# The input product of a ConvFFN by a seven-factor 2x2 block product, its activations held in DRAM

## The chip, the cores and the metric

The kernel runs on one core of one Trainium2 chip. The metric is the device time of one execution in microseconds (us). A core has five engines that each work through a queue of their own in order: TensorE (PE; the loading of its weights is shown as PEld), VectorE (DVE), ScalarE (ACT), GpSimd (POOL) and SyncE (SP, which here issues DMA transfers). They wait for one another by semaphores. SBUF is the core's memory for operands, PSUM the memory that PE writes its products to.

## The reference

One step of a hybrid layer: modulation, stick-breaking attention, a short gated convolution, a merge with an output projection, and then a feed-forward part with a convolution in it. The change concerns the last part:

```
h2 = modulate(rms_norm(x, g_norm2), shift2, scale2)
up, gate = jnp.split(h2 @ w_up, 2, axis=-1)
up_c, new_ffn = causal_dwconv(up, ffn_prev, w_fconv, b_fconv)
x = x + gate2[:, None, :] * ((jax.nn.silu(up_c) * gate) @ w_down)
```

There are 512 prompt tokens and 32 sample tokens, 1024 features, and 2816 features in the feed-forward part. All is float32.

## The kernel before

Every activation is kept with features on the partitions (128) and the T = 544 tokens as columns, in two halves of HT = 272. 1024 features are KD = 8 tiles, the 2816 are KF = 22. A float32 product is made of three products of a faster format: weights and activations are each split into a high and a low part (`split`, L91 on ACT for the high part, L92 on DVE for the low one; for weights `load_w`, L96 the transfer by SP, L99 the cast on ACT, L100 the subtraction on DVE), and `mm3` runs high by high, high by low and low by high for each contraction tile k and each half: 8 x 3 x 2 = 48 matmuls of 272 columns for a product with one weight tile.

After the output projection, `h2` makes the second norm's output for one half of the columns at a time: a product on POOL (L679), scale and shift on DVE (L682), the split into `h2h` and `h2l`. PE fills the time with the last projection tiles (`out_half`) and the first three FFN products (`up_half`: the up tiles of f = 0 and 1, the gate tile of f = 0).

The loop over f in 0..21 then does, for each tile of 128 features, the up product (48 matmuls), copies it from PSUM to `up` on ACT (L732), pads it and saves its last rows on POOL (L441 to L446), runs three taps of the convolution on DVE (L451, L453), silu on ACT (L735), the gate product (48 matmuls), multiplies the two on DVE (L739, into `gf`) and splits the result into `fh` and `fl`, which stay in SBUF. The down product follows: eight output tiles of 22 x 6 = 132 matmuls, with weights by `load_w`; the last tile is done by halves, so that the final norm of one half runs beside the other's product.

A list scheduler puts the instructions of the program on the engines' queues, so the order in the queues is not always that of the code. Tile pools with a number of buffers (`bufs`) set how far ahead an engine may run.

Of the kernel before, what the change touches and what calls it, by code (L numbers as in the profile page):

```python
# [34 lines left out]
# Token columns of every [feature, token] tile, as two halves, the latest token first:  # L35
# prompt 511..256 | sample 31..16, prompt 255..0 | sample 15..0.
# [4 lines left out]
# Columns of the per-partition vectors that are packed into one array.  # L41
# [9 lines left out]
def build(tc, a):  # L51
    nc = tc.nc
    ctx = ExitStack()
    with ctx:
# [4 lines left out]
        # ---------------------------------------------------------------- constants  # L59
# [65 lines left out]
        def proj(w, x):  # L125
            """Product with a weight tile, in DRAM or loaded."""
# [6 lines left out]
        def steps(src, post, lo):  # L133
            """The product of x with a weight tile in steps, and what follows it."""
# [10 lines left out]
        def fill(n):  # L145
            """n steps of the products that wait in the queue."""
# [7 lines left out]
        def after(inst, earlier):  # L154
            """Order two instructions of one engine."""
# [3 lines left out]
        def log_tables(earlier):  # L159
            """Load the table set that has Ln and Exp, after an activation that needs another one."""  # L160
# [6 lines left out]
        def rstd_of(pool, ss_ps, y, tables):  # L167
            """y = (mean + eps) ** -0.5 of the column sums in psum, in every partition."""
# [5 lines left out]
            # one Newton step: y * (1.5 - 0.5 v y y)  # L174
# [9 lines left out]
        # ---------------------------------------------------------------- adaLN  # L184
# [9 lines left out]
        def dot(raw, sums):  # L194
            """Each row of raw times silu(c), summed."""
# [4 lines left out]
        def ada(s, t):  # L200
            """mods[:, s, t, :]: one feature tile of one of the last four modulations, both batches."""
# [9 lines left out]
        # ---------------------------------------------------------------- first norm, first projections  # L211
# [6 lines left out]
        def flat(ps, name):  # L218
            """psum to [p, T] with all prompt columns first."""
# [9 lines left out]
        def queries(j, ps):  # L229
            """A head's (hi, lo) over each other, hi on the head's own partitions."""  # L230
# [7 lines left out]
        def keys(j, ps):  # L238
            """A head's (hi, hi) and (lo, lo)."""
# [16 lines left out]
        def values_t(j):  # L256
            """[keys, quarters]: head 0 hi, lo; head 1 lo, hi."""
# [11 lines left out]
        # sample queries, keys and values of all heads, kept until all are there  # L269
# [32 lines left out]
        def mod(s, k, on_pe):  # L302
            """mods[:, s, k, :]: one feature tile of one of the first two modulations."""
# [41 lines left out]
        # ---------------------------------------------------------------- projections and prompt attention  # L345
# [18 lines left out]
        def causal(t, width, fill):  # L364
            """Fill where the key is not before the query: [queries, blocks of width keys], last key first."""
# [4 lines left out]
        def scores(j, e):  # L370
            """One head's weights for the prompt: queries on partitions, keys from the last one back."""
# [27 lines left out]
        def transposed(sg):  # L399
            """The weights with keys on partitions, split, by rows of key blocks."""  # L400
# [441 lines left out]
```

## Time and profile before

| | us |
|---|---|
| median of 3 runs | 1123.93 |
| lowest and highest run | 1121.76, 1124.09 |
| span of the profiled execution | 1122.7 |
| PE busy | 1053.6 (94%) |
| DVE busy | 666.1 (59%) |
| ACT busy | 428.6 (38%) |
| POOL busy | 262.4 (23%) |

The span is the time from the first to the last recorded instruction of the profiled execution; of that execution no other time is recorded, and the median of the runs is 1.2 us above its span. Busy shares are averages over stages that differ: the attention lies in the first half, the FFN in the last 400 us. PE's matmuls overlap one another, so the duration of one (0.29 us) is longer than the distance between two.

### The profile page before, as it was taken

The numbers are of one execution on the slowest core, as the hardware profiler recorded it, in microseconds if no ns is written. First come the engines' busy times: TensorE is split into PE (matmuls) and PEld (weight loads), VectorE is DVE, ScalarE is ACT, GpSimd is POOL, SyncE is SP. The second block draws the span as 40 slices with busy tenths as digits, with TensorE's granted clock in tenths as the row PEclk, the third lists the DMA queues.
The fourth block names the chain that finished last, engine by engine and source line by source line (L and its number), as shares of the span: only waits on it lengthen the run. The fifth ranks groups of instructions, "written<-read, shape, count | busy, mean of one in ns | idle before, by whom it ended". The sixth has DMA issues, their size and how long they took to land.

```text
span 1122.7 us, 19599 instructions
## 1 busy us (share of the span) xinstructions
PE 1053.6 (94%) x8042; PEld 1027.6 (92%) x8042; DVE 666.1 (59%) x1005; ACT 428.6 (38%) x749; POOL 262.4 (23%) x384
## 2 busy tenths in 40 slices
PE   3898888898999999999999999899999999999995
PEld 1688787887999999999999999899999999999995
DVE  6967787776775534666677756755455455422334
ACT  5466566565643322222222253333333333322230
POOL 3434455443321101211211215300010010001112
PEclk9899999999999999999999999899999999999998
DMA  9612121211122222455455463022222222222212
GB/s 372 217 40 95 58 78 50 73 61 67 68 88 73 79 73 94 152 187 175 165 182 178 167 228 115 1 74 78 95 91 79 95 93 77 87 90 85 85 53 80
DMA packets 38153, 120.60 MB, mean 107 GB/s; under 512 B 4272, under 2 KB 7472, under 8 KB 37936
## 3 DMA queue, kind: packets, MB, share of 16 engines
q1 hardware_dynamic: 37920, 119.22, 30.9%
q8 instruction: 63, 1.03, 0.4%
q10 hardware_dynamic: 144, 0.14, 0.1%
q14 instruction: 26, 0.21, 0.1%
HBM read 112.60 MB, written 6.75 MB: 106 GB/s over the span
## 4 chain that ended last, share of the span: by engine, by line
PE 79%; DVE 10%; ACT 4%; issue 3%; POOL 2%; DMA 1%; DVEq 0%; SPq 0%; ACTq 0%; POOLq 0%
PE ps L112 72%; DVE keep L392 3%; PE o L362 2%; PE at L408 1%; POOL keep L367 1%; DVE hf L682 1%; DVE sg L393 1%; ACT keep L388 1%; DVE adum L197 1%; PE slot L112 1%; DVE kt L246 1%; DMA cbc<-in_c_dram 1%; ACT wh L99 1%; PE so L362 1%; ACT sg L389 1%
## 5 line engine op out<-in xcount | busy, mean ns | idle before, releaser
L99 ACT CAST wh<-raw 128x1024 fp32r<-128x1024 f32 x153 | 159.7, 1045 | 349.0 <-PE ps L112 246.0
L100 DVE TENSOR_TENSOR wl<-raw,wh 128x1024 fp32r<-128x1024 f32 (+1 forms) x120 | 146.4, 1222 | 169.6 <-ACT wh L99 169.0
L112 PE MATMUL ps<-hh,wh 128*128 128x272 f32 x992 | 212.0, 295 | 8.1 <-ACT qs L235 8.1
L112 PE MATMUL ps<-hl,wh 128*128 128x272 f32 x992 | 206.8, 290 | 0.0
L112 PE MATMUL ps<-hh,wl 128*128 128x272 f32 x992 | 206.6, 290 | 0.0
L112 PEld LDWEIGHTS ps<-hh,wh 128*128 128x128 f32 x992 | 157.9, 191 | 11.0 <-ACT qs L235 9.6
L112 PEld LDWEIGHTS ps<-hl,wh 128*128 128x128 f32 x992 | 157.8, 191 | 0.0
L112 PEld LDWEIGHTS ps<-hh,wl 128*128 128x128 f32 x992 | 156.9, 191 | 0.0
L112 PE MATMUL ps<-h2l,wh 128*128 128x272 f32 x704 | 150.6, 290 | 0.9 <-DVE h2l L92 0.9
L112 PE MATMUL ps<-h2h,wh 128*128 128x272 f32 x704 | 150.9, 290 | 0.3 <-ACT h2h L91 0.3
L112 PE MATMUL ps<-h2h,wl 128*128 128x272 f32 x704 | 151.1, 291 | 0.0
L100 POOL TENSOR_TENSOR wl<-raw,wh 128x1024 fp32r<-128x1024 f32 x33 | 81.9, 2481 | 203.9 <-ACT wh L99 194.3
L112 PEld LDWEIGHTS ps<-h2l,wh 128*128 128x128 f32 x704 | 113.4, 190 | 1.7 <-DVE h2l L92 1.7
L112 PEld LDWEIGHTS ps<-h2h,wh 128*128 128x128 f32 x704 | 113.6, 190 | 0.9 <-ACT h2h L91 0.8
L112 PEld LDWEIGHTS ps<-h2h,wl 128*128 128x128 f32 x704 | 112.6, 190 | 0.0
L197 DVE SCALAR_TENSOR_TENSOR adum<-araw,cbc 128x1024 f32<-128x1024 f32 x64 | 82.7, 1293 | 41.8 <-DMA araw<-in_w_ada_dram 41.0
L392 DVE TENSOR_TENSOR_SCAN keep<-keep,zero 128x512 f32<-128x512 f32 (+1 forms) x64 | 65.9, 1041 | 8.1 <-POOL keep L367 6.3
L112 PE MATMUL ps<-fl,wh 128*128 128x272 f32 x308 | 63.9, 288 | 0.0
L367 POOL TENSOR_SCALAR_AFFINE_SELECT keep<-keep 128x128 f32<-128x128 f32 x64 | 44.3, 693 | 83.5 <-issue 43.7
L112 PE MATMUL ps<-fh,wh 128*128 128x272 f32 x308 | 63.6, 288 | 0.0
L112 PE MATMUL ps<-fh,wl 128*128 128x272 f32 x308 | 63.5, 288 | 0.0
L662 POOL TENSOR_TENSOR sacc<-sacc,sq 128x272 f32<-128x272 f32 x24 | 27.5, 1162 | 143.3 <-ACT sq L660 143.3
(200 smaller groups left out, 1745.6 us busy)
## 6 DMA issues: line engine op xcount, KB each, us to landing
raw<-in_w_in_dram SPq DMA_DIRECT2D x64, 512.0 KB, 3.3
raw<-in_w_up_dram SPq DMA_DIRECT2D x44, 512.0 KB, 3.3
araw<-in_w_ada_dram SPq DMA_DIRECT2D x32, 512.0 KB, 4.0
raw<-in_w_down_dram SPq DMA_DIRECT2D x16, 512.0 KB, 3.5
mraw<-in_w_ada_dram SPq DMA_DIRECT2D x10, 512.0 KB, 7.3
raw<-in_w_branch_b_dram SPq DMA_DIRECT2D x8, 512.0 KB, 3.2
raw<-in_w_branch_a_dram SPq DMA_DIRECT2D x8, 512.0 KB, 3.3
raw<-in_w_out_dram SPq DMA_DIRECT2D x8, 512.0 KB, 3.8
```

Of the source, the lines that this page charges most:

```text
L99: nc.scalar.copy(wh[:, :nk], raw[:, :nk])
L100: lo.tensor_tensor(wl[:, :nk], raw[:, :nk], wh[:, :nk].bitcast(F32), ALU.subtract)
L112: nc.tensor.matmul(ps[:, i, 0:c1 - c0], w[:, k], x[:, k0 + k, c0:c1], start=s, stop=e)
L197: nc.vector.scalar_tensor_tensor(adum, raw, 1.0, cbc[:, n], ALU.mult, ALU.mult, accum_out=sums[:, n:n + 1])
L246: nc.vector.tensor_tensor(kt[s, e, 1], kf[s], kt[s, e, 0].bitcast(F32), ALU.subtract)
L362: nc.tensor.matmul(out, l, r, start=s, stop=t, skip_group_check=True)
L367: nc.gpsimd.affine_select(out=t, in_=t, pattern=pat, compare_op=ALU.is_gt, fill=fill, base=0, channel_multiplier=-1)
L388: nc.scalar.activation(kb, z[:, c:c + w], AF.Sigmoid, scale=-(HD ** -0.5))
L389: nc.scalar.activation(sb, z[:, c:c + w], AF.Sigmoid, scale=HD ** -0.5)
L392: nc.vector.tensor_tensor_scan(kb, kb, zero.broadcast_to([P, w]), 1.0, ALU.mult, ALU.add)
L393: nc.vector.tensor_tensor(sb, sb, kp[:, s0:s0 + w], ALU.mult)
L662: nc.gpsimd.tensor_tensor(sacc[:, c0:c1], sacc[:, c0:c1], sq, ALU.add)
```

## The change

For f = 0 and 1 the FFN works as before. For the other 20, `pair` makes the up tile and the gate tile of one f together. The weights of both are cut in two along the contraction (KH = 4 tiles each): a11 and a12 are the two parts of the up tile's, a21 and a22 of the gate tile's. The norm's output is cut by contraction half and by column half into b11, b21, b12, b22. Four sums of weights (s1 to s4, on POOL, once for each pair) and four sums of blocks (t1 to t4, once, in `sums`) then give both tiles for both halves by seven products of 4 x 3 = 12 matmuls. What is common to several results is added behind the products, from PSUM: u0 (a copy on ACT), u1 and u2 (DVE), then the gate halves `gt` (DVE) and the up halves (ACT copies L873 for one, DVE additions L877 for the other). All seven weight operands are split into high and low parts, 512 elements wide each.

The first tap moves from DVE to ACT (L832), and the product with the gate (`gf`) from DVE to POOL (L839), from `gt` in SBUF. The blocks and sums need so much of SBUF that the activations no longer fit: f = 0 to 2 are split and kept (`feh`, `fel`), f = 3 to 19 are written to DRAM (`fd`), f = 20 and 21 are kept unsplit. After the loop the 17 tiles are read back through four buffers (`fr`), split on ACT and DVE into `flh` and `fll`, and the down product reads them there. The second norm's temporaries have 16 buffers in place of 6, and the pool of the projection's weights is released earlier.

```diff
@@ second norm
-        h2h = hp.tile([P, KD, T], F32R, tag="hh", name="h2h")
-        h2l = hp.tile([P, KD, T], F32R, tag="hl", name="h2l")
+        hb = [hp.tile([P, 4, KH, HT], F32R, tag=t, name=n) for t, n in (("hh", "hbh"), ("hl", "hbl"))]
...
+        def sums():
+            for k in range(KH):
+                b11, b21, b12, b22 = hfs[0, k], hfs[0, k + KH], hfs[1, k], hfs[1, k + KH]
+                nc.vector.tensor_tensor(b11, b12, b11, ALU.subtract)
+                nc.gpsimd.tensor_tensor(b12, b22, b12, ALU.subtract)
+                nc.vector.tensor_tensor(b22, b22, b11, ALU.subtract)
+                nc.gpsimd.tensor_tensor(b21, b21, b22, ALU.subtract)
+                for name, t in (("t2", b22), ("t1", b11), ("t3", b12), ("t4", b21)):
+                    hi, lo = block(name)
+                    split(hi[:, k], lo[:, k], t, nc.gpsimd if name in ("t3", "t4") else nc.vector)
...
         up_half(1)
-        wo.release()
+        sums()
@@ operands of a pair
+            nc.sync.dma_start(r2, src2)
+            nc.sync.dma_start(r1, src1)
+            nc.gpsimd.tensor_tensor(s1, a21, a22, ALU.add)
+            nc.gpsimd.tensor_tensor(s2, s1, a11, ALU.subtract)
+            nc.gpsimd.tensor_tensor(s3, a11, a21, ALU.subtract)
+            nc.gpsimd.tensor_tensor(s4, a12, s2, ALU.subtract)
...
+                    nc.scalar.copy(h[:, ks_], t)
+                    nc.vector.tensor_tensor(l_[:, ks_], t, h[:, ks_].bitcast(F32), ALU.subtract)
...
+            put(wp, "w", 2, ("a11", a11), ("a12", a12))
+            put(swp, "g1", 2, ("s2", s2), ("s1", s1))
+            put(swp, "g2", 1, ("s3", s3), ("a22", a22))
+            put(swp, "g3", 1, ("s4", s4))
@@ a pair
+            product(pa, "a11", "b11", True)
+            nc.scalar.copy(u[0], pa)
+            product(pb, "s2", "t2", True)
+            nc.vector.tensor_tensor(u[1], pb, u[0], ALU.add)
+            product(pc, "s1", "t1", True)
+            product(pb, "s3", "t3", False)
+            nc.vector.tensor_tensor(u[2], pb, u[0], ALU.add)
+            second_1(pc, u[2])
+            product(pa, "a12", "b21", False)
+            first_0(pa)
+            product(pb, "a22", "t4", False)
+            second_0(pb, u[0])
+            product(pc, "s4", "b22", False)
+            first_1(pc, u[1])
@@ activation
-            cv = conv(ftp.tile([P, T + 2], F32, tag="cv", bufs=1, name="fcv"), up, "wf", "bf", f)
-            last = nc.scalar.activation(cv, cv, AF.Silu)
...
+            nc.scalar.activation(cv, up[:, 0:T + 2], AF.Identity, scale=V("wf", 3 * f + 2), bias=V("bf", f))
+            for n in (1, 2):
+                nc.vector.scalar_tensor_tensor(cv, up[:, n:n + T + 2], V("wf", 3 * f + 2 - n), cv, ALU.mult, ALU.add)
+            lastact[0] = nc.scalar.activation(cv, cv, AF.Silu)
...
+            eng = nc.vector if f < 2 else nc.gpsimd
+            for s_, d, c_ in zip(parts(gt), parts(two(gf)), padded(cv)):
+                eng.tensor_tensor(d, s_, c_, ALU.mult)
+            if f < NE:
+                split(feh[:, f], fel[:, f], gf)
+            elif f < KF - 2:
+                nc.sync.dma_start(fd[:, f], gf)
+            else:
+                ftail[f] = gf
@@ after the loop
+        for f in range(NE, KF):
+            if f in ftail:
+                raw = ftail[f]
+            else:
+                raw = ffp.tile([P, T], F32, tag="fr", bufs=4, name="fr")
+                nc.sync.dma_start(raw, fd[:, f])
+            split(flh[:, f - NE], fll[:, f - NE], raw)
```

In the middle of the FFN, ACT's queue before holds, for one f, two casts of weights, the split of the f before, the up copies and silu (`ps` is the product's PSUM tile, `fcv` the convolution's row, the numbers tell tiles of one name apart):

```order
L99 CAST wh_9064<-raw_9062 128x1024
L732 COPY up_8990<-ps_8941 128x512
L732 COPY up_8990<-ps_8941 128x32
L735 ACTIVATE fcv_8997<-fcv_8997 128x546
L99 CAST wh_9131<-raw_9129 128x1024
L91 CAST fh_7828<-gf_9057 128x544
```

After, ACT's queue in the middle of the loop holds for one pair (`ab_10373` is the PSUM tile of this pair's products, `fcv_10326` the row of the pair before, and the casts are of operands one and two pairs ahead):

```order
L832 ACTIVATE fcv_10326<-up_10188,vec_75 128x546
L788 CAST g1h_10651<-s1_10637 128x512
L835 ACTIVATE fcv_10326<-fcv_10326 128x546
L788 CAST g1h_10651<-s2_10638 128x512
L788 CAST wh_10645<-raw1_10633 128x512
L873 COPY up_10335<-ab_10373 128x256
L873 COPY up_10335<-ab_10373 128x16
L788 CAST wh_10645<-raw1_10633 128x512
L788 CAST g2h_10510<-s3_10492 128x512
L788 CAST g2h_10510<-raw2_10487 128x512
L788 CAST g3h_10516<-s4_10493 128x512
```

The up copies of a pair now stand behind silu of the pair before and behind a cast of an operand of two pairs ahead.

POOL's queue before holds for one f only the pads and the last rows of the up tile:

```order
L441 MEMSET up_10006 128x2
L442 COPY up_10006<-vec_75 128x2
L445 COPY newf_77<-up_10006 128x2
L446 COPY newf_77<-up_10006 128x2
L441 MEMSET up_10133 128x2
L442 COPY up_10133<-vec_75 128x2
```

After, at the same place of the loop, POOL has for one pair:

```order
L780 TENSOR_TENSOR s3_10492<-raw1_10486,raw2_10487 128x512
L781 TENSOR_TENSOR s4_10493<-raw1_10486,s2_10491 128x512
L441 MEMSET up_10482 128x2
L442 COPY up_10482<-vec_75 128x2
L839 TENSOR_TENSOR gf_10331<-gt_10191,fcv_10326 128x2x256
L839 TENSOR_TENSOR gf_10331<-gt_10191,fcv_10326 128x2x16
L779 TENSOR_TENSOR s2_10638<-s1_10637,raw1_10633 128x512
L778 TENSOR_TENSOR s1_10783<-raw2_10780 128x512
L445 COPY newf_77<-up_10335 128x2
L446 COPY newf_77<-up_10335 128x2
```

The product `gf` of the pair before stands ahead of the sum s2 that ACT's cast `g1h_10651<-s2_10638` reads.

DVE's queue before, one f in the middle of the loop:

```order
L100 TENSOR_TENSOR wl_9386<-raw_9383,wh_9385 128x1024
L92 TENSOR_TENSOR fl_7829<-gf_9311,fh_7828 128x544
L100 TENSOR_TENSOR wl_9446<-raw_9443,wh_9445 128x1024
L451 TENSOR_SCALAR fcv_9378<-up_9371,vec_75 128x546
L453 SCALAR_TENSOR_TENSOR fcv_9378<-up_9371,vec_75,fcv_9378 128x546 x2
L739 TENSOR_TENSOR gf_9438<-ps_9389,fcv_9378 128x2x256
L739 TENSOR_TENSOR gf_9438<-ps_9389,fcv_9378 128x2x16
```

After, the same engine for the pair whose ACT and POOL rows stand above (from u1 to the up halves):

```order
L816 TENSOR_TENSOR u1_10376<-ab_10373,u0_10375 128x272
L834 SCALAR_TENSOR_TENSOR fcv_10326<-up_10188,vec_75,fcv_10326 128x546
L789 TENSOR_TENSOR g1l_10652<-s1_10637,g1h_10651 128x512
L819 TENSOR_TENSOR u2_10377<-ab_10373,u0_10375 128x272
L881 TENSOR_TENSOR gt_10338<-pc_10374,u2_10377 128x272
L789 TENSOR_TENSOR g1l_10652<-s2_10638,g1h_10651 128x512
L789 TENSOR_TENSOR wl_10646<-raw1_10633,wh_10645 128x512 x2
L880 TENSOR_TENSOR gt_10338<-ab_10373,u0_10375 128x272
L789 TENSOR_TENSOR g2l_10511<-s3_10492,g2h_10510 128x512
L877 TENSOR_TENSOR up_10335<-pc_10374,u1_10376 128x256
L877 TENSOR_TENSOR up_10335<-pc_10374,u1_10376 128x16
```

The second tap of the pair before stands behind u1 of this pair, and seven splits of 512 have taken the place of two of 1024.

## Rows read from the trace of the kernel before

**Rows 1.** The chain that ended last, by engine and by line.

```profile
PE 79%; DVE 10%; ACT 4%; issue 3%; POOL 2%; DMA 1%; DVEq 0%; SPq 0%; ACTq 0%; POOLq 0%
PE ps L112 72%; DVE keep L392 3%; PE o L362 2%; PE at L408 1%; POOL keep L367 1%; DVE hf L682 1%; DVE sg L393 1%; ACT keep L388 1%; DVE adum L197 1%; PE slot L112 1%; DVE kt L246 1%; DMA cbc<-in_c_dram 1%; ACT wh L99 1%; PE so L362 1%; ACT sg L389 1%
```

**Rows 2.** Stretches: us, PE, PEld, DVE, ACT, POOL busy (instructions), PEclk, DMA, GB/s.

```profile
707.00:710.00 3.00, 3.00 (x15) 2.99 (x14) 2.82 (x9) 1.45 (x4) 0.06 (x1) 0.50 0.00 0
840.00:880.00 40.00, 40.00 (x321) 40.00 (x321) 19.79 (x28) 13.22 (x20) 3.55 (x14) 1.00 0.27 93
1000.00:1040.00 40.00, 40.00 (x321) 40.00 (x320) 10.18 (x15) 9.98 (x13) 4.88 (x4) 1.00 0.29 86
```

**Rows 3.** Timeline of ACT: start, duration, instruction, idle time before and its releaser.

```profile
722.56 0.68 ACT L732 COPY up<-ps 128x512 f32<-128x512 f32 x2 [1.55 <-PE ps L112]
...
862.32 0.66 ACT L732 COPY up<-ps 128x512 f32<-128x512 f32 x2
865.96 0.66 ACT L735 ACTIVATE fcv<-fcv 128x546 f32<-128x546 f32 x1 [2.98 <-DVE fcv L453]
...
874.34 0.66 ACT L732 COPY up<-ps 128x512 f32<-128x512 f32 x2
```

**Rows 4.** Groups of instructions, 740 to 960 us: busy us, mean ns, idle.

```profile
L100 DVE TENSOR_TENSOR wl<-raw,wh 128x1024 fp32r<-128x1024 f32 x37 | 45.3, 1225 | 79.2 <-ACT wh L99 78.8
...
L453 DVE SCALAR_TENSOR_TENSOR fcv<-up,vec,fcv 128x546 f32<-128x546 f32 x36 | 28.4, 789 | 2.5
...
L92 DVE TENSOR_TENSOR fl<-gf,fh 128x544 fp32r<-128x544 f32 x18 | 12.9, 719 | 0.0
...
L735 ACT ACTIVATE fcv<-fcv 128x546 f32<-128x546 f32 x18 | 11.9, 662 | 53.6 <-DVE fcv L453 53.6
L91 ACT CAST fh<-gf 128x544 fp32r<-128x544 f32 x18 | 11.7, 650 | 0.9
```

**Rows 5.** Groups of instructions 272 wide, 680 to 880 us.

```profile
L679 POOL TENSOR_TENSOR hf<-xr,rs 128x272 f32<-128x272 f32 x16 | 12.4, 802 | 10.9 <-DVE rs L177 9.9 <-DVE h2l L92 1.0
...
L92 DVE TENSOR_TENSOR h2l<-hf,h2h 128x272 fp32r<-128x272 f32 x16 | 7.0, 467 | 0.1
L91 ACT CAST h2h<-hf 128x272 fp32r<-128x272 f32 x16 | 6.7, 417 | 14.4 <-DVE hf L682 14.1
```

**Rows 6.** Groups of POOL's instructions, 460 to 640 us.

```profile
L100 POOL TENSOR_TENSOR wl<-raw,wh 128x1024 fp32r<-128x1024 f32 x15 | 35.9, 2391 | 133.8 <-ACT wh L99 124.1 <-DMA raw<-in_w_branch_a_dram 9.6
```

**Rows 7.** Timeline of DVE: at 24, 571, 720, 735 and 864 us.

```profile
24.08 5.40 DVE L331 TENSOR_TENSOR xt<-xt,y 128x544 f32<-128x544 f32 x3
...
571.49 1.96 DVE L197 SCALAR_TENSOR_TENSOR adum<-araw,cbc 128x1024 f32<-128x1024 f32 x1 [1.65 <-DMA araw<-in_w_ada_dram]
...
574.02 1.21 DVE L197 SCALAR_TENSOR_TENSOR adum<-araw,cbc 128x1024 f32<-128x1024 f32 x1
...
720.53 0.96 DVE L92 TENSOR_TENSOR h2l<-hf,h2h 128x272 fp32r<-128x272 f32 x2
...
735.36 0.79 DVE L739 TENSOR_TENSOR gf<-ps,fcv 128x512 f32<-128x512 f32 x2 [2.48 <-PE ps L112]
...
864.25 1.61 DVE L453 SCALAR_TENSOR_TENSOR fcv<-up,vec,fcv 128x546 f32<-128x546 f32 x2
```

**Rows 8.** Timeline of POOL, at 23 and at 570 us.

```profile
23.09 7.58 POOL L331 TENSOR_TENSOR xt<-xt,y 128x544 f32<-128x544 f32 x4 [1.81 <-DVE y L177]
...
569.98 2.39 POOL L100 TENSOR_TENSOR wl<-raw,wh 128x1024 fp32r<-128x1024 f32 x1 [9.63 <-ACT wh L99]
```

**Rows 9.** Timeline of PE at the first norm product of the second half.

```profile
705.90 0.72 PE L669 MATMUL ssh<-sq,ones 128*128 128x272 f32 x2 [1.77 <-ACT sq L660]
```

**Rows 10.** DMA issues: KB each, median us from issue to landing.

```profile
xr<-in_x_dram SPq DMA_DIRECT2D x8, 272.0 KB, 4.3
out_y_dram<-xr SPq DMA_DIRECT2D x4, 272.0 KB, 2.6
```

More of the change, by code (lines that the diff above doesn't have):

```diff
@@ L726, in build @@
-        fl = ffp.tile([P, KF, T], F32R, name="fl")
-        for f in range(KF):
-            ps = first[f][1] if f in first else proj(a["w_up"][f], (h2h, h2l))
-            up = ftp.tile([P, T + 4], F32, tag="up", bufs=1, name="up")
+        ftp = tc.alloc_tile_pool(name="ftmp", bufs=1)
+        swp = tc.alloc_tile_pool(name="sweights", bufs=1)
+        fdp = ctx.enter_context(tc.tile_pool(name="fdram", bufs=1, space=bass.MemoryType.DRAM))
+        fd = fdp.tile([P, KF, T], F32, name="fd")
+        NE = 3
@@ new lines, in pair, with product @@
+        def pair(src1, src2, second_0, second_1, first_0, first_1):
+            w = operands(src1, src2)
+            ab = pmm.tile([P, 2, 512], F32, tag="mm", name="ab")
+            pa, pb = ab[:, 0, 0:HT], ab[:, 1, 0:HT]
+            pc = pss.tile([P, 512], F32, tag="ss", name="pc")[:, 0:HT]
+            def product(ps, wn, xn, s):
+                (wh, wl), (xh, xl) = w[wn], block(xn)
+                for k in range(KH):
+                    for n, (wt, xs) in enumerate(((wh, xh), (wh, xl), (wl, xh))):
+                        nc.tensor.matmul(ps, wt[:, k], xs[:, k], start=s and k == 0 and n == 0,
+                                         stop=k == KH - 1 and n == 2, skip_group_check=True)
+            u = [ftp.tile([P, HT], F32, tag=f"u{n}", bufs=2, name=f"u{n}") for n in range(3)]
+            product(pa, "a11", "b11", True)
[12 more added lines that the diff above has]
+            first_1(pc, u[1])
@@ L730, in build, with up_row @@
+        lastact = [None]
+        def up_row(f):
+            up = ftp.tile([P, T + 4], F32, tag="up", bufs=2, name="up")
             pads(up, V("sf", 2 * f, 2))
+            return up
+        for f in range(2):
+            ps = first[f][1]
+            up = up_row(f)
             for src, d in zip(parts(ps), padded(up)):
                 nc.scalar.copy(d, src)
-            last_rows(newf[:, f], up)
-            cv = conv(ftp.tile([P, T + 2], F32, tag="cv", bufs=1, name="fcv"), up, "wf", "bf", f)
@@ L735, in build @@
-            last = nc.scalar.activation(cv, cv, AF.Silu)
-            ps = first[KF][1] if f == 0 else proj(a["w_up"][KF + f], (h2h, h2l))
-            gf = ftp.tile([P, T], F32, tag="gf", bufs=1, name="gf")
-            for s_, d, c_ in zip(parts(ps), parts(two(gf)), padded(cv)):
-                nc.vector.tensor_tensor(d, s_, c_, ALU.mult)
-            split(fh[:, f], fl[:, f], gf)
-        nc.sync.dma_start(a["newf"], newf)
+            if f == 0:
+                gt = first[KF][1]
+            else:
+                gt, w = acc(), load_w(a["w_up"][KF + f])
+                for i in range(2):
+                    plain(gt, w, i)
@@ new lines, in build @@
+        nc.sync.dma_start(a["newf"], newf)
+        last = lastact[0]
+        for p in (swp, ftp, exp_):
+            p.release()
+        ffp = ctx.enter_context(tc.tile_pool(name="ffn", bufs=1, side="right"))
+        flh = ffp.tile([P, KF - NE, T], F32R, name="flh")
+        fll = ffp.tile([P, KF - NE, T], F32R, name="fll")
+        for f in range(NE, KF):
+            if f in ftail:
+                raw = ftail[f]
+            else:
+                raw = ffp.tile([P, T], F32, tag="fr", bufs=4, name="fr")
+                nc.sync.dma_start(raw, fd[:, f])
+            split(flh[:, f - NE], fll[:, f - NE], raw)
@@ L743, in build, with __init__, __getitem__ @@
+        class Cat:
+            def __init__(self, e, l_):
+                self.e, self.l_ = e, l_
+            def __getitem__(self, at):
+                p, k, c = at
+                return self.e[p, k, c] if k < NE else self.l_[p, k - NE, c]
+        fh, fl = Cat(feh, flh), Cat(fel, fll)
         steps = [(k0, min(KD, KF - k0)) for k0 in range(0, KF, KD)]
```

69 lines of the change are left out of this document (60 added, 9 removed).

## The prediction

> **What bounds the kernel now.** I read the chain of waits first. TensorE (PE) holds 79% of it, and the product line L112 alone 72% [rows 1]: the kernel ends when PE has done its matmuls. Next, the span cut into stretches: in the FFN (840 to 880, and 1000 to 1040 for the down product) PE is busy for 40.00 us of 40.00 at full granted clock, with 321 matmuls in each [rows 2], so one costs 40/321 = 0.1246 us and nothing delays it. There VectorE (DVE) is busy 19.79 us of 40, ScalarE (ACT) 13.22, GpSimd (POOL) 3.55. One f (up tile and gate tile, 96 matmuls of each half, 11.96 us by that pitch) takes 874.34 - 862.32 = 12.02 us between two copies of the up tile [rows 3]. So the question has two sides: how many matmuls go away, and whether the three slower engines, with much more to do for each f, still stay hidden.
>
> **What is removed.** A pair has 7 products x 4 k x 3 = 84 matmuls in place of 96. Twenty pairs lose 240 matmuls: 240 x 0.1246 = **-29.9 us** if PE never waits. PE's own time for a pair is 84 x 0.1246 = 10.5 us.
>
> **What a pair adds.** The durations are read from the groups of instructions: ACT 544 wide 0.65, DVE split 544 wide 0.72, DVE tap 0.79, silu 0.66 [rows 4]; 272 wide ACT 0.42, DVE 0.47, POOL 0.80 [rows 5]; POOL 1024 wide 2.39 [rows 6]. No row has POOL alone on 512 elements; between 272 and 1024 it comes to 0.80 + 240/752 x 1.59 = 1.31, and I take 1.28 (1024 halved gives 1.20, which is the floor). ACT at 512 wide is taken as 0.60.
>
> POOL then has, for each pair, four operand sums and one gf product of that size and small copies: 5 x 1.28 + about 0.6 = 7.0 us. DVE has 7 splits (half of the 1.22 of 1024 wide [rows 4], 0.6 each), two taps (1.6), three additions of 272 (0.45 each) and the two for the up row (0.65): about 8 us. ACT has 7 casts (4.2), u0, up copies, first tap, silu: about 6.7 us. Each by itself is under 10.5, so by busy time alone the change would pay.
>
> **Why I do not take it.** The engines run their queues in order, and in the order shown above they form a ring through one pair. Follow it from u1 (L816). DVE adds u1 (0.45) and then runs the second tap of the pair before (0.79); ACT's silu of that pair waits for the tap (0.66); POOL's gf (L839) waits for the silu (1.28, and 0.2 for the 16 columns); the next row of POOL's queue is s2 of two pairs ahead (1.28); ACT's next cast is of that s2 and then wh (2 x 0.60); only behind them stand the up copies L873 (0.66 for both [rows 3]); the a22 product may write into the same PSUM tile only after those copies; and PE runs a22 (12), the rest of s4 (4), a11 and s1 of the next pair (7 + 5) and its s2 (12), 40 x 0.1246 = 4.98 us, until the next u1 can start. The sum is 0.45 + 0.79 + 0.66 + 1.48 + 1.28 + 1.20 + 0.66 + 4.98 = 11.50. Five hand-overs lie in the ring; one is seen at 0.10 us, a tap that ended at 864.25 + 1.61 = 865.86 and a silu that began at 865.96 [rows 3, 7]; with 0.2 for the end of PE's last matmul that makes 0.7. **Without any contention the ring takes 12.2 us**, already more than the 12.02 of before.
>
> **Contention.** With two inputs from SBUF, DVE and POOL do not run beside each other. POOL began a split at 569.98 and ended it at 572.37 [rows 8]; a DVE instruction that began at 571.49 inside it took 1.96 us, the same one alone 1.21 at 574.02 [rows 7]: it did its work from the time POOL ended. At 23 us the two engines alternate: four POOL products of 544 in 7.58 us, three DVE ones beside them in 5.40, 1.80 each against the 0.72 that a DVE split of 544 takes [rows 4, 7, 8]. In the ring the tap, gf and s2 are of that kind, and beside them DVE has 7 splits for each pair. Each of the three can find the other engine at work: nothing at best, at worst the whole of it (gf and s2 behind a split, 0.55 each, the tap behind a POOL sum, 1.2: 2.3). I take 0.8, a third of that, since the other engine is busy for about half the time and the wait is then half of an instruction. So a pair is **13.0 us, bounds 12.2 and 14.5**, and 20 pairs cost 20 x (13.0 - 12.02) = **+19.6 us** (the 29.9 saved is in it). The additions u1, u2, gt and up have one input in PSUM and are free of it.
>
> The Trainium skill, "SBUF — State Buffer", section "Who interferes with whom", says that a DVE instruction with two SBUF inputs contends with a GpSimd instruction that reads SBUF, that the one which starts first holds the shared ports for its whole duration, and that the other blocks fully. It speaks against putting the sums on POOL beside DVE's splits. By this rule each of the three waits could be a whole instruction, and the pair would be the 14.5 of the upper bound; by the alternation of the rows it lies between.
>
> **The start of the FFN.** Before, DVE ends the norm's splits at 721.49 and the up copy starts at 722.56 [rows 3, 7]; PE runs on with up f=1, and the gate of f=1 ends at 735.36, where DVE's product that waited for it begins [rows 7], so it starts near 735.36 - 6.0 = 729.4. After, DVE and POOL each have 16 instructions of 272 for the sums, all with two SBUF inputs, from 720.5 on, and ACT's up copy stands behind their 16 casts. At 272 a DVE and a POOL instruction that alternate cost 0.47 + 0.80 less their overlapping starts, 1.0: 16 us, to 736.5, where PE's gate f=1, which waits for that copy, would have started at 729.4: +7. PE then finds half clock: after 1.77 us of idle time ahead of 705.90 [rows 9] the stretch from 707 was granted 0.50 of full clock, the lower of its two levels [rows 2], which over 3 us costs 1.5. The pairs' first sums on POOL stand behind the same 16, another +3 (0 to 6). Together **+12 us** (6 to 16).
>
> **The passage to the down product.** The first load of fr waits for POOL's last gf. From the end of PE's last pair: up 0.65, first tap 0.66, two taps 1.6, silu 0.66, gf 1.48, hand-overs 0.6 = 5.6 us; then the load. A transfer of 272 KB takes 2.6 as y leaves, 4.3 when x comes in beside weights [rows 10]; I take 2.6, as the queues are half empty here. With the cast 0.65 PE can go on at 9 us, having had 18 matmuls (2.2). Then 17 tiles come in through 4 buffers, each used for 2.6 + 0.65 + 0.72 + 0.2 = 4.17 us: one each 1.04, where PE needs 6 x 0.125 = 0.75. The last of the 17 is there at 9 + 16 x 1.04 = 25.6; with it and two more PE is at 28, against 22 x 0.75 = 16.4 before: **+11.5 us** (8 to 19 with 4.3). The stores to DRAM and the earlier output of the norm lie beside this and are put at nothing: SP issues one more transfer per pair, which waits for gf; if a raw load behind it came late, a pair would wait for it, and that is inside the 14.5.
>
> **Sum.** 19.6 + 12 + 11.5 = +43 on a span of 1122.7, 1165.8. The median of the runs shown, 1123.93, is 1.2 above the span: **1167, and I write 1168 us** (half clock after waits of some pairs).
>
> **Rivals.** (a) The ring has no contention: 12.2 us a pair, 16 us less: 1152. For it speaks that POOL and DVE are in a fixed order and can settle into gaps; against it, the alternation at 23 us. (b) The ring is not closed, because POOL's 512 sums are much faster than taken, or because silu and gf run far enough ahead: PE sets the pair, 10.5 us, and with the two passages -31 + 12 + 11.5 = -7: 1117, faster. It decides at 12.02 - 23.5/20 = 10.8 us a pair. Against it: the ring's PE, ACT and DVE parts alone are 8.7, and two POOL instructions would have to take 2.1 with their hand-overs. (c) Every wait is a whole instruction, or PE's waits within each pair (1.8 us and more) lower the clock, as 1.77 us did [rows 2, 9]: 14.5 us a pair, 1198.
>
> **How the numbers follow.** The forecast (12.5 to 13.8 us a pair) has 0.55, its own range 1155 to 1184. (a) has 0.17, (c) 0.13, (b) 0.11, and 0.04 is left for a pair of about 10.8 that ends where it was. Faster by over 0.2% (what a measurement of this kernel can tell) is (b), 0.11; within it 0.04; slower 0.85. The range for 8 in 10 leaves out (b) and the end of (c): 1130 to 1196.
>
> **What will show it.** Right: PE's a22 product with about 1.8 us of idle time ahead in every pair, released by ACT's up copies; pairs 13.0 us apart; DVE splits longer than 0.6 where a POOL sum overlaps; a gap of 7 us before the gate of f=1; flh casts about 1 us apart at the start of the down product, after a gap of near 7 us on PE. Wrong: PE gapless through the pairs at 10.5 us (then (b)), POOL's sums well under 1.2 us, or the up copies early and another wait before a22. If the pairs are right and the total is not, the two passages are at fault.

## The result: 4.3% slower, and the profile after

The changed kernel takes 1171.74 us (median of 4 runs, 1170.16 to 1173.67) against 1123.58 before on the same chips: a ratio of 1.0429, 95% interval 1.0412 to 1.0447. The forecast was 1168 us. The profiled execution has a span of 1171.6 us, 48.9 more than before.

First the parts of the page that answer to [rows 1]: busy time by engine, and the chain that ended last.

```profile
PE 1052.2 (90%) x7802; PEld 1008.4 (86%) x7802; DVE 772.4 (66%) x1179; ACT 488.9 (42%) x907; POOL 429.3 (37%) x520
...
PE 54%; DVE 20%; POOL 8%; ACT 7%; issue 7%; DMA 4%; POOLq 0%; DVEq 0%; ACTq 0%; SPq 0%
```

PE has 240 matmuls less (7802 against 8042) but its share of the chain has fallen from 79% to 54%: the chain now runs for long stretches through DVE, POOL and ACT. The stretches of the span (columns as in [rows 2]) show where PE is not busy.

```profile
720.00:760.00 40.00, 29.02 (x178) 27.69 (x179) 33.10 (x46) 19.38 (x42) 31.63 (x38) 0.79 0.12 40
...
840.00:880.00 40.00, 34.54 (x253) 32.26 (x253) 30.32 (x46) 18.64 (x40) 26.29 (x32) 1.00 0.29 101
...
1000.00:1040.00 40.00, 28.66 (x182) 26.23 (x181) 21.92 (x34) 19.19 (x30) 4.04 (x6) 0.83 0.52 163
1040.00:1080.00 40.00, 40.00 (x320) 40.00 (x320) 12.40 (x21) 11.89 (x17) 4.87 (x4) 1.00 0.31 89
```

In the loop of pairs PE is busy 34.54 us of 40, where it had 40.00 [rows 2], at full clock; DVE rose from 19.79 to 30.32 and POOL from 3.55 to 26.29. At the start of the FFN and at the start of the down product PE stands still for about 11 us of 40 each, and there the granted clock falls too. From 1040 on all is as before.

The span's growth splits at three places that the trace of PE gives. The gate of f = 1 ends at 735.4 before [rows 7] and 747.4 after: +12.0. From there to the end of the last pair it is 263.3 us, against 20 x 12.02 = 240.4: +22.9. From there to the end of the span 160.9, against 1122.7 - 735.4 - 240.4 = 146.9: +14.0. The forecast had 12, 19.6 and 11.5.

One pair in the middle of the loop, on POOL, ACT and DVE (timelines, columns as in [rows 3]):

```profile
859.37 1.76 POOL L781 TENSOR_TENSOR s<-raw,s 128x512 f32<-128x512 f32 x1 [1.23 <-DVE g3l L789]
...
862.49 1.50 POOL L839 TENSOR_TENSOR gf<-gt,fcv 128x512 f32<-128x512 f32 x2
863.95 1.29 POOL L779 TENSOR_TENSOR s<-s,raw 128x512 f32<-128x512 f32 x1
...
869.97 1.29 POOL L780 TENSOR_TENSOR s<-raw,raw 128x512 f32<-128x512 f32 x1 [2.19 <-DVE g2l L789]
```

```profile
861.75 0.66 ACT L835 ACTIVATE fcv<-fcv 128x546 f32<-128x546 f32 x1 [1.08 <-DVE fcv L834]
865.27 0.62 ACT L788 CAST g1h<-s 128x512 fp32r<-128x512 f32 x1 [2.86 <-POOL s L779]
865.79 0.61 ACT L788 CAST wh<-raw 128x512 fp32r<-128x512 f32 x1
866.31 0.44 ACT L873 COPY up<-ab 128x256 f32<-128x256 f32 x2
...
868.54 0.62 ACT L788 CAST g2h<-s 128x512 fp32r<-128x512 f32 x1 [1.26 <-PE ab L809]
...
879.41 0.44 ACT L873 COPY up<-ab 128x256 f32<-128x256 f32 x2
```

```profile
859.91 0.43 DVE L816 TENSOR_TENSOR u<-ab,u 128x272 f32<-128x272 f32 x1
860.27 1.45 DVE L834 SCALAR_TENSOR_TENSOR fcv<-up,vec,fcv 128x546 f32<-128x546 f32 x1
...
870.22 1.59 DVE L789 TENSOR_TENSOR g2l<-raw,g2h 128x512 fp32r<-128x512 f32 x1
871.73 0.68 DVE L789 TENSOR_TENSOR g3l<-s,g3h 128x512 fp32r<-128x512 f32 x1
872.33 0.77 DVE L834 SCALAR_TENSOR_TENSOR fcv<-up,vec,fcv 128x546 f32<-128x546 f32 x1
873.03 0.43 DVE L816 TENSOR_TENSOR u<-ab,u 128x272 f32<-128x272 f32 x1
```

And PE at the a22 product of that pair:

```profile
866.81 0.39 PE L809 MATMUL ab<-exh,g2h 128*128 128x272 f32 x1 [1.31 <-ACT up L873]
```

This is the ring of the prediction, instruction by instruction: the second tap (860.27), silu (861.75), gf (862.49), s2 (863.95), its cast (865.27), wh, the up copies (866.31), and PE, idle for 1.31 us until those copies are done. (Between the tap and gf the chain of waits names POOL's pads of the next up row in place of silu: both wait for the tap, and the pads end at 862.36, silu at 862.41.) From one up copy to the next it is 879.41 - 866.31 = 13.10 us, where 13.0 was forecast. The second tap takes 1.45 us in place of 0.77 because POOL's s4, begun at 859.37, holds until 861.13.

The chain of waits through the same pair (start, duration, what) corrects one arc of the ring:

```profile
866.41 0.35 ACT up L873 x2
866.76 0.04 issue
866.81 1.65 PE ab L809 x11
...
868.54 0.63 ACT g2h L788
...
869.80 0.50 DVE up L877 x2
870.30 1.50 DVE g2l L789
871.80 0.60 DVE g3l L789
872.40 0.70 DVE fcv L834
873.10 0.14 DVE u L816
```

Behind the a22 product the chain does not go on through PE's next 28 matmuls to u1, as I had it. It goes to ACT's cast of the next s3, which waits for a22 because `g2` has one buffer, and from there through DVE's queue: the low part of s3, the up halves, the low part of a22 (1.59 us, since POOL's s3 had begun at 869.97, 0.25 us before it; the uncontended split behind it, of s4, takes 0.68), the first tap, and only then u1, for which PE's s2 product had been done since 872.3. ACT's cast of s3, too, waits for a neighbour: it writes the half of `g2` that PE had read by 862.2, and a22 reads the other half. No run tried two tiles there.

PE's idle times understate what a pair loses, because matmuls overlap. From start to start, a22's first matmul comes 1.60 us behind the one before it and the next 0.22 later, where 0.125 is the pitch: 1.6 us lost. The s3 product loses 0.6 in the same way (for u1), the s2 and the a12 product 0.2 each (behind u0's copy and u2). With PE's 10.5 that is the whole 13.1.

### The profile page after: what moved, and what is told of

Its sections match the earlier page's. It is cut to its first block, busy times and chain, and to the rows that moved or that the text cites. A ratio compares the mean times of both kernels' runs of the same rounds, so it can differ in the third digit from the quotient of the medians.

```text
span 1171.6 us, 19712 instructions
## 1 busy us (share of the span) xinstructions
PE 1052.2 (90%) x7802; PEld 1008.4 (86%) x7802; DVE 772.4 (66%) x1179; ACT 488.9 (42%) x907; POOL 429.3 (37%) x520
## 4 chain that ended last, share of the span: by engine, by line
PE 54%; DVE 20%; POOL 8%; ACT 7%; issue 7%; DMA 4%; POOLq 0%; DVEq 0%; ACTq 0%; SPq 0%
PE ps L112 44%; DVE fcv L834 4%; PE ab L809 4%; DVE keep L392 3%; DVE g2l L789 2%; POOL gf L839 2%; PE o L362 2%; POOL s L779 2%; DMA fr<-fd 1%; PE at L408 1%; POOL keep L367 1%; DVE sg L393 1%; DMA araw<-in_w_ada_dram 1%; DVE hf L693 1%; DVE adum L197 1%
## 5 line engine op out<-in xcount | busy, mean ns | idle before, releaser
L99 ACT CAST wh<-raw 128x1024 fp32r<-128x1024 f32 (+1 forms) x113 | 117.5, 1041 | 241.7 <-PE ps L112 134.6
L100 DVE TENSOR_TENSOR wl<-raw,wh 128x1024 fp32r<-128x1024 f32 (+1 forms) x80 | 97.2, 1217 | 80.0 <-ACT wh L99 79.5
L809 PE MATMUL ab<-exh,g2h 128*128 128x272 f32 x160 | 50.1, 313 | 30.8 <-ACT up L873 22.4
L392 DVE TENSOR_TENSOR_SCAN keep<-keep,zero 128x512 f32<-128x512 f32 (+1 forms) x64 | 65.9, 1040 | 8.2 <-POOL keep L367 6.3
L112 PE MATMUL ps<-flh,wh 128*128 128x272 f32 x266 | 56.7, 295 | 10.6 <-ACT flh L91 10.6
L789 DVE TENSOR_TENSOR g1l<-s,g1h 128x512 fp32r<-128x512 f32 x40 | 36.5, 913 | 44.9 <-ACT g1h L788 44.7
L809 PEld LDWEIGHTS ab<-exh,g2h 128*128 128x128 f32 x160 | 30.0, 187 | 39.3 <-ACT up L873 26.7
L112 PE MATMUL ps<-fll,wh 128*128 128x272 f32 x266 | 56.7, 295 | 0.7 <-DVE fll L92 0.6
L112 PE MATMUL ps<-flh,wl 128*128 128x272 f32 x266 | 55.9, 292 | 0.0
L834 DVE SCALAR_TENSOR_TENSOR fcv<-up,vec,fcv 128x546 f32<-128x546 f32 x44 | 50.2, 1142 | 5.0 <-ACT up L858 3.9
L112 PEld LDWEIGHTS ps<-flh,wh 128*128 128x128 f32 x266 | 43.0, 194 | 11.4 <-issue 8.4
```

What stands on the lines that cost most here:

```text
L99: nc.scalar.copy(wh[:, :nk], raw[:, :nk])
L100: lo.tensor_tensor(wl[:, :nk], raw[:, :nk], wh[:, :nk].bitcast(F32), ALU.subtract)
L112: nc.tensor.matmul(ps[:, i, 0:c1 - c0], w[:, k], x[:, k0 + k, c0:c1], start=s, stop=e)
L392: nc.vector.tensor_tensor_scan(kb, kb, zero.broadcast_to([P, w]), 1.0, ALU.mult, ALU.add)
L789: nc.vector.tensor_tensor(l_[:, ks_], t, h[:, ks_].bitcast(F32), ALU.subtract)
L809: nc.tensor.matmul(ps, wt[:, k], xs[:, k], start=s and k == 0 and n == 0, stop=k == KH - 1 and n == 2, skip_group_check=True)
```

## Experiments

Three theories were to be told apart for the pairs. **Ring**: a pair lasts as long as the ring of waits above, contention being a part of it. **Exclusion by load**: DVE's two-SBUF instructions and POOL's together fill 12.7 of the 13.1 us, and every wait is only where that shows. **Casts**: ACT's queue sets it. All kernels below are the changed kernel with one edit, or with several where it is said; the time beside each is to be held against its 1171.74. A time with a range is the median of four runs, one without a range is a single run. The pair's length is the distance between two u0 copies in the middle of the loop, from the trace.

**e1, own PSUM tiles.** The wait of a22 on the up copies isn't one of data: the copies read bank a of the tile `ab`, a22 writes bank b. They share a tile, and the program's waits are made by tiles.

```diff
...
-            pa, pb = ab[:, 0, 0:HT], ab[:, 1, 0:HT]
+            bb = pm3.tile([P, 2, 512], F32, tag="mm", name="bb")
+            pa, pb = ab[:, 0, 0:HT], bb[:, 0, 0:HT]
```

> The a and b accumulators of a pair get PSUM tiles of their own, so that the a22 product no longer waits for the up copies. Ring theory: PE leaves the ring; what is left runs from the second tap over silu, gf, s2, its cast, the up copies, four more casts and the first tap back to the second tap, about 12.0 us a pair (11.5 to 12.6) in place of 13.1: about 1150 us (1140 to 1162). Rival, exclusion: DVE's two-SBUF instructions (5.6 us a pair) and POOL's (7.1) fill 12.7 of the 13.1 us, so the wait on the copies only shows it, and the time stays at 1164 to 1172.

1155.44 us (1153.75 to 1156.31), ratio to before 1.0297 (1.0279 to 1.0314): 16.3 us less, 12.1 us a pair. Exclusion by load, which allowed 8 us at most and has 12.7 us of work a pair, falls. In the new pair DVE is fuller (36.68 of 40 us at 880 to 920) and PE waits twice, 0.41 us for u1 and 0.58 for u2, of 12.09; the wait for the up copies is gone.

The number is the ring's, its path is not. With the new tile the scheduler also changed the order: POOL now runs s2 ahead of gf, so gf no longer stands ahead of s2 as the expectation had it, and the chain goes from s2's cast and low part to u2 and on through PE's products.

```profile
890.07 1.30 POOL L780 TENSOR_TENSOR s<-s,raw 128x512 f32<-128x512 f32 x1
891.32 2.38 POOL L841 TENSOR_TENSOR gf<-gt,fcv 128x512 f32<-128x512 f32 x2
```

So the 16.3 us are those of the second tile and of the order that came with it, and no run parts the two; that 12.0 was expected and 12.1 came is luck.

**e4, no weight sums.**

```diff
...
-            nc.gpsimd.tensor_tensor(s1, a21, a22, ALU.add)
...
-            nc.gpsimd.tensor_tensor(s4, a12, s2, ALU.subtract)
+            s1, s2, s3, s4 = a21, a22, a11, a12
```

> Leaves out the four sums of weights on POOL (the products take raw quarters in their place). Ring theory: s2 (1.28) and the second tap's wait for s4 (0.7) leave the ring, 11.1 us a pair, and the start loses 2 us: about 1129 us. Rival, exclusion alone sets the pair: nothing is left to exclude, PE sets 10.5, about 1117. Rival, ACT's casts set the pair: 1165 to 1172.

1132.57 us, 11.12 us a pair: the ring's number (11.1), but again not by the ring. PE is busy 40.00 us of 40 and the chain of waits holds nothing but PE's products: PE sets the pair.

```profile
840.00:880.00 40.00, 40.00 (x305) 38.38 (x304) 28.98 (x53) 21.49 (x44) 10.90 (x24) 1.00 0.33 123
```

Its matmuls are 305 here, where e14 below has 320. Three times in a pair their starts stand about 0.2 us farther apart than the pitch, ahead of the s2, a12 and a22 products (859.59, 853.15, 855.86), each of which writes one bank of `ab` just behind a read of the other; e14, with two tiles, has none of the three. That is 0.6 us on PE's 10.5. By the chain shown above, the ring without the sums would have lost the block of a22's low part (0.9) as well and come to 10.2, below PE's own time; the expectation did not have that block, and its 11.1 was met by luck. As this kernel takes away the ring's sum and the exclusion together, it doesn't tell the two apart. It shows that the sums cost 39 us and that ACT's casts, of which none is gone, don't set the pair.

**e3, no s4**, and **e3d, s4 as a write.** The first leaves s4 out and lets the scheduler order the rest:

```diff
-            nc.gpsimd.tensor_tensor(s4, a12, s2, ALU.subtract)
+            s4 = a12
```

> Leaves out only the sum s4 (its product takes a raw quarter). s4 is not in the ring, but the second tap waits 0.7 us for it. Ring theory: 12.4 us a pair, about 1157 us (1154 to 1160). Rival, exclusion by total load: POOL has 1.28 less, 11.8 us, about 1146. Rival, the tap's wait doesn't matter: 1170 to 1173.

1171.57 us: no change, and the ring's 1157 missed. The trace shows why. The second tap is at 0.77 us, as expected, but without s4 the scheduler put s1 between gf and s2 on POOL, and in most pairs it put the casts of both sums ahead of the up copies on ACT, so that two sums stand in the ring in place of one (gf at 857.97, s1 at 859.41, s2 at 860.78, the up copies at 863.14):

```profile
857.97 1.49 POOL L839 TENSOR_TENSOR gf<-gt,fcv 128x512 f32<-128x512 f32 x2 [0.40 <-ACT fcv L835]
859.41 1.29 POOL L778 TENSOR_TENSOR s<-raw 128x512 f32<-128x512 f32 x1
860.78 1.28 POOL L779 TENSOR_TENSOR s<-s,raw 128x512 f32<-128x512 f32 x1
```

```profile
860.74 0.62 ACT L788 CAST g1h<-s 128x512 fp32r<-128x512 f32 x1 [2.85 <-POOL s L778]
862.10 0.62 ACT L788 CAST g1h<-s 128x512 fp32r<-128x512 f32 x1 [0.74 <-POOL s L779]
862.62 0.61 ACT L788 CAST wh<-raw 128x512 fp32r<-128x512 f32 x1
863.14 0.44 ACT L873 COPY up<-ab 128x256 f32<-128x256 f32 x2
```

These pairs take 13.3 to 13.8 us. In the others the cast of s2 comes behind the up copies, one sum stands in the ring, and they take 12.4, which is the ring's number. What was gained at the tap was given back by the order. The second kernel therefore keeps the order of POOL's queue by hand and puts a memset in s4's place, which only writes SBUF:

```diff
...
-            nc.gpsimd.tensor_tensor(s4, a12, s2, ALU.subtract)
+            nc.gpsimd.memset(s4, 0.5)
...
+                after(i2, gfs[turn[0] - 1])
```

> The sum s4 on POOL becomes a memset of the same tile (its product takes a constant), which writes SBUF and reads none, and the order of POOL's queue is held as in the changed kernel (gf, then s2 of two pairs ahead). Ring theory with exclusion: the second tap's wait for s4 (0.7 us) goes and nothing else of the ring changes, 12.4 us a pair, about 1157 us (1154 to 1161). Rival, exclusion by total load sets the pair: 11.8, about 1146. Rival, the tap's wait is no part of what limits: 1169 to 1173, as without s4 in another order.

1158.48 us, 12.42 us a pair in every pair. In its DVE timeline the first tap runs beside POOL's memset, and the second (864.84) starts when the memset is over:

```profile
863.79 0.77 DVE L839 SCALAR_TENSOR_TENSOR fcv<-up,vec,fcv 128x546 f32<-128x546 f32 x1
...
864.84 0.77 DVE L839 SCALAR_TENSOR_TENSOR fcv<-up,vec,fcv 128x546 f32<-128x546 f32 x1
```

```profile
863.92 0.53 POOL L786 MEMSET s<- 128x512 f32 x1 [1.21 <-DVE g3l L794]
```

The memset ends at 864.45, before the first tap does (864.56), where s4 was held by that tap and ran into the second. So one block of 0.68 us is worth 0.68 us in each pair and 13 us in all. Here the order of POOL's queue is that of the changed kernel (gf, s2, s1, s3, then the memset), so this is the experiment that tests the ring by itself. The load theory wanted 11.8 us a pair for this kernel.

**e2, gf on DVE.**

```diff
-            eng = nc.vector if f < 2 else nc.gpsimd
+            eng = nc.vector
```

> gf goes back to DVE. Ring theory: gf (1.49) and s2 (1.29) leave the ring, since ACT's silu and casts no longer wait for POOL's gf; the next bound is DVE's and POOL's load or PE, 10.8 to 11.6 us a pair: about 1134 us (1126 to 1142). Rival, exclusion by total load: POOL 1.49 less, DVE 0.8 more, 12.4 us a pair, about 1158.

1175.35 us (1174.33 to 1176.48), ratio to before 1.0472 (1.0456 to 1.0487): a little slower, and both numbers missed: most pairs take 13.4 us. ACT's casts no longer wait for gf, but another ring closed: gf now stands ahead of u2 on DVE, waits for silu and meets POOL's s2 there, and a12 waits for u2.

```profile
862.55 1.83 DVE L839 TENSOR_TENSOR gf<-gt,fcv 128x512 f32<-128x512 f32 x2
```

```profile
864.79 0.40 PE L809 MATMUL ab<-hbh,wh 128*128 128x272 f32 x1 [1.31 <-DVE u L819]
```

That wait is again one of the shared tile: u2 reads bank b, a12 writes bank a. With e1's edit a12 needn't wait for u2, which the next run tests.

**e9, own PSUM tiles and gf on DVE** (both edits).

> Own PSUM tiles for the a and b accumulators and gf on DVE, together. If gf on DVE alone lost because PE's a12 waited for u2 behind gf (a wait that the shared PSUM tile makes), it can't lose here: POOL has 1.5 us less, DVE 0.8 more, and the chain of DVE that sets the pair there (taps, u1, low parts, u2) stays: 11.6 to 12.1 us a pair, about 1150 us (1145 to 1156). Rival, gf on DVE is dear by itself: slower than with own PSUM tiles alone, 1160 or more.

1149.73 us (1148.53 to 1150.70), ratio 1.0236 (1.0216 to 1.0256), 11.70 us a pair. The same edit that cost 3.6 us in e2 gains 5.7 over e1 here (medians; by the ratios, since the runs are of different chips, 4.8 and 6.9). Here too the scheduler's order changed with the tile (on DVE the second tap now stands ahead of u1), so the gain is of both together.

**e5, no sums of blocks.**

```diff
-        sums()
+        for old, new in (("b11", "t1"), ("b21", "t2"), ("b22", "t3"), ("b12", "t4")):
+            BLOCK[new] = BLOCK[old]
```

> Leaves out the sums of blocks at the start (the products take the plain blocks t for t). Start theory: the 7.8 us gap ahead of the gate of f = 1 and the half clock behind it go, and the first weight sums start earlier: 12 to 14 us less, about 1159 us (1156 to 1162). Rival, the start waits for the weights of the first pair: 1168 or more.

1164.93 us: 6.8 less, half of the 12 to 14. The gap ahead of the gate of f = 1 is gone and that gate ends at 734.7, but PE then stands idle for 6.5 us in the first pair (736.93 to 743.43):

```profile
743.43 0.60 PE L810 MATMUL ab<-hbh,g1h 128*128 128x272 f32 x1 [6.50 <-ACT u L815]
```

The s2 product's operand is there from 736.0 on, but it writes the tile `ab` that ACT's copy of u0 reads, and that copy (743.00) stands in ACT's queue behind the next pair's casts, which wait for POOL's sums, and behind the split of a gf.

**e7, early up copy.** The copy of f = 0 waited for memory that the sums still read; here it writes into two tiles that nothing else uses at that time.

```diff
...
-            up = ftp.tile([P, T + 4], F32, tag="up", bufs=2, name="up")
+            up = upf[f] if f < 2 else ftp.tile([P, T + 4], F32, tag="up", bufs=2, name="up")
...
+            with tc.high_priority():
+                for src, d in zip(parts(ps), padded(up)):
+                    nc.scalar.copy(d, src)
```

> The up rows of f = 0 and 1 are put in two tiles of their own, in place of memory that the sums of blocks still read, and ACT's copy of f = 0 goes ahead of most of the sums' casts. Start theory: the copy waited for that memory and for the casts; PE's gate of f = 1 then starts near 729 at full clock, and the first pair waits for the weight sums behind the block sums: first steady pair about 5 us earlier, 1167 us (1162 to 1169). Rival, the first pair's operands set the start alone: 1170 to 1173.

1172.89 us (1171.78 to 1175.43), ratio 1.0449 (1.0431 to 1.0468): no gain. The gate ends at 736.1, 11 us earlier, and PE then waits 9.57 us (736.11 to 745.67) at the first product of the first pair, for DVE's first gf, which reads a gate tile in PSUM and stands behind taps and splits that contend with POOL's sums. The rival's number was right, and the gap moved one step on. The edit gives the rows tiles of their own and puts the copies ahead; which of the two moved the gate wasn't tried.

**e6, no way through DRAM.**

```diff
...
-            elif f < KF - 2:
-                nc.sync.dma_start(fd[:, f], gf)
...
-            split(flh[:, f - NE], fll[:, f - NE], raw)
...
-                return self.e[p, k, c] if k < NE else self.l_[p, k - NE, c]
+                return self.e[p, k % NE, c]
```

> Leaves out the way through DRAM (no stores, no loads, no splits after the loop; the down product reads the three kept tiles again and again). Passage theory: the down product starts at once, 13 to 14 us less, about 1158 us (1155 to 1161). Rival, the stores also slow the loop's weight loads: pairs below 13.1 us and less than 1153. Rival, the passage is hidden: 1168 or more.

1156.79 us, 15.0 less; pairs at 13.10 us as ever, so the stores cost the loop nothing.

**e8, six buffers**, and **e12, six buffers with own PSUM tiles.**

```diff
-                raw = ffp.tile([P, T], F32, tag="fr", bufs=4, name="fr")
+                raw = ffp.tile([P, T], F32, tag="fr", bufs=6, name="fr")
```

> Six buffers for the tiles read back from DRAM in place of four, nothing else. Passage theory: the 17 tiles come in at the pace of the buffers; a buffer is taken for about 5 us (transfer 3.6, cast, subtraction), so the pace goes from about 1.07 to 0.85 us a tile, still over PE's 0.75: about 3 us less, 1168 us (1166 to 1170). Rival, DRAM or the queue sets the pace: 1170 to 1173.

1168.23 us (1167.05 to 1169.47), ratio 1.0400 (1.0377 to 1.0424): 3.5 less.

> Own PSUM tiles and six buffers, together; the gains add if they lie in different stages: 1155.4 less 3, about 1152 us (1150 to 1155). Rival, the six buffers gain nothing: 1154 to 1157.

1150.41 us (1149.59 to 1151.35), ratio 1.0243 (1.0224 to 1.0262): 5.0 less than e1. The two gains add (16.3 and 3.5; together 21.3).

**e14, the products alone**: own PSUM tiles, and the edits of e4, e5 and e6 together.

> Leaves out the sums of blocks, the sums of weights and the way through DRAM, with own PSUM tiles: the seven products and what is added behind them, against what the sums cost. If the 29.9 us of matmuls are really saved and only the rest takes them back, PE runs gapless at 10.5 us a pair but for the start: 1095 to 1103 us. Rival, the products lose by themselves (their additions from PSUM, or DVE's and ACT's casts): over 1108.

1096.82 us, 26.8 less than before. The stretch that stood at 34.54 us of PE above:

```profile
840.00:880.00 40.00, 40.00 (x320) 40.00 (x319) 31.91 (x57) 23.94 (x47) 10.30 (x24) 1.00 0.32 106
```

PE is gapless at 10.6 us a pair, with all casts, splits and additions still there. The saving of the matmuls is real; the sums, the way through DRAM and the waits that come with them and with the shared tile take it back and 48 us more. Of the kernels that leave nothing out none came below the kernel before; the nearest, e9, is 2.4% above it. And with the same casts on ACT as in the changed kernel, the theory that ACT's queue sets the pair falls too.

## Why the prediction was right, step by step

**The matmuls saved (29.9 us).** Right: e14 shows 26.8 of it once the sums, the passage and the shared tile are gone.

**The ring (13.0 us a pair, 12.2 without contention).** Right in its length, 13.10, and in the wait that shows it, a22 on the up copies; PE's idle time there is 1.31 us, not the 1.8 named; from start to start the copies cost PE 1.6 of the 2.6 us above 10.5, u1 0.6, and u0's copy and u2 0.2 each. e3d moves the pair by what the ring says (12.4), and so do the pairs of e3 with one sum. e1 and e4 met the ring's numbers (12.1, 11.1) on other paths and don't count for it. One arc was wrong: from a22 to u1 I had PE's next 28 matmuls, about 3.5 us with their end; the chain of waits shows ACT's cast of s3 and DVE's queue there, from 868.5 to 873.0.

**Contention (0.8 us, between 0 and 2.3).** The sum held for a reason other than mine. I let the tap, gf and s2 meet the other engine by chance, a third of the worst case. In fact the order repeats exactly, so that nothing is by chance: gf (1.50 with its 16 columns) and s2 (1.29) meet nobody, the tap is blocked in every pair by s4 (0.68), and the low part of a22, which I did not have in the ring, by s3 (0.9). Beside PE's 3.5 us the arc by DVE takes 4.5 with the 0.9 in it. Without its two blocks the measured ring would be 13.1 - 0.68 - 0.9 = 11.5, not 12.2: the chain from the tap to the up copies takes about 0.7 less than my terms, where I had added hand-overs to durations that may hold them already. So contention was put too low by 0.8 and the rest too high by 0.7, and that 13.0 came out is in part luck.

The rule that the prediction weighed, of the Trainium skill, "SBUF — State Buffer", section "Who interferes with whom", says also that a GpSimd instruction which only writes is no hindrance. e3d agrees as far as it goes: the memset (0.53 us) and the first tap (0.77) run side by side and neither waits, where s4, begun in the same tap, took 1.76. A tap that starts while a memset runs is not in the trace. That the one which starts first holds for its whole duration is what the tap at 860.27 shows, which ended 0.59 us after s4's end at 861.13.

**The start (+12).** The gate of f = 1 ended 12.0 us later, but my sum has only 8.5 up to there (7 of gap, 1.5 of half clock) and put the other 3 behind it, where 1.3 came (22.9 less 20 x 1.08). The gap was 7.8 us against 7. DVE and POOL alternated at 0.93 us, where 1.0 was taken. PE came to the gap 1.6 us later than before, since it ran at 0.50 from 720 to 726, where the kernel before had 0.58 and 0.85. And half clock lasted from the gate's start at 738.84 to about 743.9, and so cost about 2.5 us, not 1.5:

```profile
738.00:741.00 3.00, 2.16 (x9) 2.16 (x10) 0.89 (x1) 2.89 (x7) 2.94 (x9) 0.50 0.00 0
741.00:744.00 3.00, 3.00 (x16) 3.00 (x15) 3.00 (x3) 0.75 (x2) 2.92 (x4) 0.52 0.03 8
```

And the sums of blocks are worth only 6.8 of it (e5): behind them stand waits in the first pairs, for which I had put 3 us of first weight sums and which show when the sums are gone (6.5 us idle, for u0's copy) or passed by (9.57, for DVE's gf, e7).

**The passage (+11.5).** The mechanism was right and the term too small, because it left out the clock and a second hole: +14.0, or 15.0 by e6. From the end of the last pair at 1010.7 to the end of gf it took 5.7 us (5.6 forecast), the first load 2.7 (2.6):

```profile
1014.92 1.46 POOL L839 TENSOR_TENSOR gf<-gt,fcv 128x512 f32<-128x512 f32 x2 [5.08 <-ACT fcv L835]
```

```profile
1016.42 1.19 ACT L91 CAST flh<-gf 128x544 fp32r<-128x544 f32 x2 [0.27 <-POOL gf L839]
1019.07 1.37 ACT L91 CAST flh<-fr 128x544 fp32r<-128x544 f32 x2 [1.47 <-DMA fr<-fd]
...
1033.45 2.72 ACT L91 CAST flh<-fr 128x544 fp32r<-128x544 f32 x4 [2.92 <-DMA fr<-fd]
```

```profile
1019.82 0.79 PE L112 MATMUL ps<-flh,wh 128*128 128x272 f32 x2 [8.22 <-ACT flh L91]
```

PE waited 8.2 us, not 6.8, since the matmuls that I let it run meanwhile had mostly been run among the last pair's. Behind that gap PE again ran at half clock (0.50 granted from 1020 to 1023 us). The transfers took 3.6 us (median of the 17), not 2.6, and yet the pace through the four buffers was the forecast one: eleven loads were issued in 10.97 us, 1.0 each.

```profile
1016.41 10.97 SPq L896 DMA_DIRECT2D fr<-fd  x11
```

Then a load of weights stands between the eleventh and the twelfth tile on SP's queue, ACT's casts have a hole of 2.92 us before 1033.45, PE waits 2.03 us at 1034.15, and half clock follows again:

```profile
1035.00:1038.00 3.00, 3.00 (x15) 3.00 (x16) 1.93 (x3) 2.04 (x3) 0.00 (x0) 0.60 0.62 182
```

Added up: 8.2 of gap, 3.0 in four later waits, about 3.5 at half clock in the two stretches, less 1.4 for the 11 matmuls run earlier, is 13.3 of the 14.0. Six buffers, which also put all 17 loads ahead of the weights and took them to 0.84 us each (14.35 us for 17), gave 3.5 us back; pace and order weren't tried apart.

**The rivals.** No contention, PE as the bound of a pair, and whole waits everywhere: none came. The half clock that one of them feared in the loop did not come with PE's 1.3 us gaps (granted clock 1.00 from 760 to 1000). It came behind the gaps of 7.8 and 8.2 us and the wait of 2.03, and at 720 behind waits of at most 0.3 us among few matmuls (9 from 717 to 720).

## What to carry to other kernels

Taking a tenth of the matmuls off an engine that is always busy pays only if what makes it possible has a place of its own: count for each helper not its busy time but the ring of queued instructions that one period has to run through, because an in-order queue makes a neighbour's cast or sum a part of the path. A wait that the data doesn't need, as between two banks of one PSUM tile, can close such a ring; two tiles in place of one, with the order that the scheduler then chose, were worth 16 us here, and decided whether another edit gained 5.7 us or lost 3.6. And once a scheduler sets the order, any edit may move instructions into the ring or out of it (e3, e1): hold the order when one cost is to be measured, and read the chain again before a number that came true is called a proof. PE "busy" all the time (e4) may still lose 5% between its starts.

## What the runs showed that was not expected

Contention between DVE and POOL in a loop of fixed order is no average: the same instructions were blocked in every pair by the same time (the tap 0.68 us, the low part of a22 0.9, and, outside the chain, the low part of s2), and others, gf and s2 among them, in none. A POOL sum of 512 elements took 1.29 us when nothing blocked it, as estimated, and 1.76 when DVE was ahead of it. A memset of that size on POOL took 0.53 us beside a tap that had begun before it, and neither was held.
